# Low parts of weights made by an accumulating DMA instead of a subtraction, in a two-layer decoder trunk

## The chip, the cores and the metric

One core of a Trainium2 chip runs the kernel. The metric is the device time of one execution in microseconds (us), the lower the better. The profile names the engines PE (TensorE, matrix products; PEld is its weight load), DVE (VectorE), ACT (ScalarE), POOL (GpSimd) and SP (SyncE, which here only issues DMAs).

## The reference

A decoder trunk of two layers works on 512 tokens of 1024 features in fp32. Layer 0 mixes a gated linear recurrence with a sparse attention, layer 1 is multi-head latent attention. Both end alike:

```python
h = layer_norm(DN_ALPHA * x + m, ln1_g[i], ln1_b[i])            # m: the mixer's output
f = jnp.square(jax.nn.relu(h @ mlp_w1[i])) @ mlp_w2[i]          # 1024 -> 4096 -> 1024
e = jax.nn.sigmoid(h @ ple_w_gate[i]) * (p[i] @ ple_w_proj[i])
x = layer_norm(DN_ALPHA * h + f + e, ln2_g[i], ln2_b[i])
```

Layer 1 begins with a down-projection and makes its queries from it:

```python
down = x @ w_down                                               # 1024 -> 512 + 256 + 32
cq, ckv, kr = jnp.split(down, [MLA_Q_LORA, MLA_Q_LORA + MLA_KV_LORA], axis=-1)
q = (rms_norm(cq, q_norm) @ w_uq).reshape(bsz, s, MLA_HEADS, MLA_NOPE + MLA_ROPE)
...
q_rope = rope(q_rope, cos[:, None, :], sin[:, None, :])
```

## The kernel before, in words

Activations lie transposed, features on the 128 partitions and 512 tokens along the free dimension, eight tiles of 128 features. A product in fp32 quality is made of three products in the faster fp32r type: each operand is split into a high part `hi`, its value rounded to fp32r, and a low part `lo`, the value less `hi`. `mm3` (lines 106 to 109) adds hi x hi (line 107), hi x the activation's lo (108) and the weight's lo x hi (109) in PSUM; lines 916 to 918 and 977 to 979 do the same in the other orientation.

`wload` (lines 92 to 104) brings one weight block of 128x2048, 1 MB, from HBM into a tile `wraw` by a DMA on SP's queue, and `split` makes the parts in two pieces of 128x1024 (in four where `pieces=4`): ScalarE casts the piece into `whi` (line 89), then VectorE, or GpSimd where `sub=nc.gpsimd.tensor_sub`, subtracts `whi` from `wraw` into `wlo` (line 90). The tiles `wraw`, `whi` and `wlo` have two buffers each, shared by all weights of the kernel. A buffer of `whi` and `wlo` comes free when TensorE has done the last product with the block before the last, a buffer of `wraw` when its last split has read it, and only then can SP issue the next load into it.

The order of instructions on each engine is made when the program is built, by a list scheduler that goes by priorities and its own estimates of time; it keeps dependencies, not the order of the code. `high_priority(ahead)` puts the splits of a block that many places forward. On the chip each engine works through its own list in order.

The feed-forward (`mlp`, line 848) runs in four parts per layer. Each part makes 1024 of the 4096 hidden features in four blocks of `mlp_w1` by `seven` (lines 737 to 823; a form with seven products in place of eight, with splits of its own at lines 758 and 759 and a third pair of weight buffers), and multiplies them by four blocks of `mlp_w2` in `gemm_t` (line 895), adding into `y`. With eight parts there are 32 blocks of `mlp_w2`; a block takes 48 matmuls of 512 columns. In the fourth part the last block is computed in two halves of the tokens (`tail`), so that the second layer norm (`Norm`, lines 201 to 330) can begin on the first half. That norm sums on VectorE (lines 245 and 257), takes the sums to TensorE (274) and applies the result (318, 319, 327, 328; line 330 on GpSimd).

Layer 1's mixer begins with `group_n` (lines 905 to 920) for `w_dn0` (512 columns) and `w_dn1` (288 columns), each in two blocks of four pieces with GpSimd subtracting, and goes on with the rotary weight `w_qr` (line 971), one block of two pieces, also with GpSimd.

Of the kernel before, what the change touches and what calls it, by code (L numbers as in the profile page):

```python
# [12 lines left out]
OP = mybir.AluOpType  # L13

P = 128
S = 512
# [37 lines left out]
def hybrid_kernel(ctx: ExitStack, tc: tile.TileContext, a: dict, out: bass.AP):  # L54
    nc = tc.nc
    uid = [0]

    def nm(s):
        uid[0] += 1
        return f"{s}_{uid[0]}"  # L60

    def pool(name, bufs=2):
        return tc.tile_pool(name=name, bufs=bufs, reuse_waits="tile")
# [6 lines left out]
    def f(ap):  # L70
        return ap.bitcast(F32)
# [16 lines left out]
    def split(hi, lo, src, act=None, sub=None):  # L88
        (act or nc.scalar.copy)(hi, src)  # L89
        (sub or nc.vector.tensor_sub)(lo, src, f(hi))  # L90

    def wload(dram, idx, n=2048, pieces=2, sub=None, raw=None, ahead=30):

        hi = wp.tile([P, 2048], F32R, tag="whi", name=nm("whi"))
        lo = wp.tile([P, 2048], F32R, tag="wlo", name=nm("wlo"))
        if raw is None:
            raw = wp.tile([P, 2048], F32, tag="wraw", name=nm("wraw"))
            nc.sync.dma_start(raw[:, :n], dram[idx, :, :n])
        m = n // pieces
        with tc.high_priority(ahead):  # L100
            for i in range(pieces):
                c = slice(i * m, (i + 1) * m)
                split(hi[:, c], lo[:, c], raw[:, c], sub=sub)
        return hi, lo

    def mm3(ps, whi, wlo, xhi, xlo, start, stop):
        nc.tensor.matmul(ps, whi, xhi, start=start, stop=False)  # L107
        nc.tensor.matmul(ps, whi, xlo, start=False, stop=False)  # L108
        nc.tensor.matmul(ps, wlo, xhi, start=False, stop=stop)  # L109
# [1 line left out]
    ALL, HALVES = slice(0, S), (slice(0, H), slice(H, S))  # L111

    def gemm_t(dram, idxs, xs, evac, kk=8, nt=2, lead=0, ps=ps_tile, sub=None, loaded=None,
               halves=(), tail=0, ahead=30):

        tiles = {}  # L120

        def part(g, c, w, kn, cs=ALL):
            ktot = kk * len(idxs[g])
            for k, n in kn:
                key = g, n, cs.start
                if key not in tiles:
                    tiles[key] = ps()
                kx = c * kk + k
                hi, lo = xs[kx]
                o = slice((k * nt + n) * P, (k * nt + n + 1) * P)  # L130
                mm3(tiles[key][:, cs], w[0][:, o], w[1][:, o], hi[:, cs], lo[:, cs],
                    kx == 0, kx == ktot - 1)
                if kx == ktot - 1:
                    evac(g * nt + n, tiles[key], cs)

        first, last = 0, len(idxs) - tail
        byn = [(k, n) for n in range(nt) for k in range(kk)]
        byk = [(k, n) for k in range(kk) for n in range(nt)]
        if lead:
            w = loaded or [wload(dram, idxs[g][0], sub=sub, ahead=ahead) for g in range(2)]  # L140
            first = 2
            for cs in HALVES if "lead" in halves else (ALL,):
                for k in range(lead):
                    for g in range(2):
                        part(g, 0, w[g], [(k, n) for n in range(nt)], cs)
                for g in range(2):
                    kn = (byk, byn)[g]
                    part(g, 0, w[g], [t for t in kn if t[0] >= lead], cs)
        for g in range(first, last):
            for c, idx in enumerate(idxs[g]):  # L150
                part(g, c, wload(dram, idx, sub=sub, ahead=ahead), byn)
        if tail:
            w = {(g, c): wload(dram, idx, sub=sub, ahead=ahead) for g in range(last, len(idxs)) for c, idx in enumerate(idxs[g])}
            for cs in HALVES:
                for g in range(last, len(idxs)):
                    cn = [(c, n) for n in range(nt) for c in range(len(idxs[g]))]
                    for c, n in cn if cs.start == 0 else sorted(cn):
                        part(g, c, w[g, c], [(k, n) for k in range(kk)], cs)
# [12 lines left out]
    for k in range(KT):  # L171
        c = slice(k * 256, (k + 1) * 256)
# [283 lines left out]
    def mixer0(mixed):  # L456
        with pool("m0", 1) as m0, pool("m0s") as sc:
# [58 lines left out]

            kt = []
            gemm_t(a["w_in"], [[1], [0]], x, ev0, lead=8, loaded=w0)


# [327 lines left out]
    def mlp(layer, norm1, pp, mp):  # L848
        h, xb, pools = norm1.h, [], ExitStack()
        third = pools.enter_context(pool(f"third{layer}"))  # L850


        def evg(n, ps, cs):
            sg = mp.tile([P, S], F32, tag=f"ah{n % 2}", bufs=1, name=nm("sg"))[:, cs]
            nc.scalar.activation(sg, ps[:, cs], AF.Tanh, scale=0.5)
            nc.vector.scalar_tensor_tensor(pp[n][:, cs], sg, 1.0, pp[n][:, cs], op0=OP.add, op1=OP.mult)
            if n == 3 and cs.start:
                xb.extend(norm1.sums(mp))
            for i in range(4) if n == 3 and cs.start else (n,) if n > 3 else ():
                nc.vector.scalar_tensor_tensor(y[i], y[i], ALPHA, pp[i], op0=OP.mult, op1=OP.add)  # L860

        gemm_t(a["w_gate"], [[layer * 4 + g] for g in range(4)], h, evg, lead=8, halves=("lead",), ahead=120)
        for part in range(4):
            act = []

            def ev1(g, c11, t):
                nc.scalar.activation(t[:, :H], c11, AF.Relu)
                nc.scalar.activation(t[:, H:], t[:, H:], AF.Relu)
                nc.scalar.activation(t, t, AF.Square)
                for i in range(2):  # L870
                    n, r = 2 * g + i, t[:, i * S:(i + 1) * S]
                    hi = mp.tile([P, S], F32R, tag=f"ah{n}", bufs=1, name=nm("ah"))
                    lo = mp.tile([P, S], F32R, tag=f"al{n}", bufs=1, name=nm("al"))
                    split(hi, lo, r)
                    act.append((hi, lo))

            seven(a["mlp_w1"], [layer * 16 + part * 4 + g for g in range(4)], xb, mp, ev1, third=third)

            def ev2(n, ps, cs):
                yn = y[n][:, cs]  # L880
                if part == 0:
                    nc.vector.scalar_tensor_tensor(yn, ps[:, cs], norm1.ab[:, n:n + 1], yn, op0=OP.add, op1=OP.add)
                else:
                    nc.vector.tensor_add(yn, yn, ps[:, cs])  # L884
                if part == 3:
                    if n == 3:
                        norm.first()
                    elif n > 3:
                        norm.add(n, cs)

            if part == 3:
                pools.close()
                norm = Norm(pools.enter_context(pool(f"norm{layer}b", 1)), layer, 1, final=layer == 1)
            b = (layer * 2 + part // 2) * 8 + part % 2
            gemm_t(a["mlp_w2"], [[b + 2 * g] for g in range(4)], act, ev2, tail=part == 3)
        pools.close()
        return norm.h


    def mixer1(x1, mixed):  # L900
        with pool("m1", 1) as m1, ExitStack() as pools:
# [3 lines left out]
            def group_n(dram, ncols, xs, evac):  # L905

                ps = [ps_tile() for _ in range(NB)]
                w = [[u[:, :4 * ncols].rearrange("p (k n) -> p k n", n=ncols)
                      for u in wload(dram, ci, 4 * ncols, pieces=4, sub=nc.gpsimd.tensor_sub)] for ci in range(2)]
                for half in range(2):  # L910
                    for k in range(KT):
                        for b in (2 * half, 2 * half + 1):
                            c = slice(b * P, (b + 1) * P)
                            o = ps[b][:, :ncols]
                            (hi, lo), (whi, wlo) = xs[k], (u[:, k % 4] for u in w[k // 4])
                            nc.tensor.matmul(o, hi[:, c], whi, start=k == 0, stop=False)  # L916
                            nc.tensor.matmul(o, hi[:, c], wlo, start=False, stop=False)  # L917
                            nc.tensor.matmul(o, lo[:, c], whi, start=False, stop=k == KT - 1)  # L918
                    for b in (2 * half, 2 * half + 1):
                        evac(b, ps[b])  # L920
# [47 lines left out]


            qr = m1.tile([P, NB, MLA_H, 32], F32, tag="qr", name="qr")  # L970
            whi, wlo = (w.rearrange("p (k n) -> p k n", n=S) for w in wload(a["w_qr"], 0, sub=nc.gpsimd.tensor_sub))
            for b in range(NB):
                ps = ps_tile()
                c = slice(b * P, (b + 1) * P)
                for k in range(4):
                    hi, lo = cq[k]
# [241 lines left out]
```

## Time and profile before

| | |
|---|---|
| median of 3 runs (lowest, highest) | 1265.72 us (1263.74, 1266.52) |
| the profiled execution: its time, its span | 1267.45 us, 1265.7 us |
| busy: PE, DVE, ACT, POOL | 1225.8, 924.4, 667.1, 167.4 us |
| mean granted clock of PE | 0.990 |

The span runs from the first to the last instruction of the profiled execution. Busy time is the sum over an engine's instructions; engines work side by side, so these don't add up. The granted clock is TensorE's, as a share of 2.4 GHz; its lower level is 1.2 GHz. In a row `out<-in` are the program's names for tiles, `L90` is line 90, and in brackets stands how long the engine was idle before an instruction and what ended that.

### The profile page before, as it was taken

Reading aid. Unit: us, or ns where it says so; the run is one execution under the profiler, and the core shown is the slowest. Engines: PE = TensorE matmul, PEld = TensorE weight load, DVE = VectorE, ACT = ScalarE, POOL = GpSimd, SP = SyncE. Lnnn points to the kernel's source line nnn. Section 1 sums busy time; section 2 is a strip of 40 time slices with the busy share of each in tenths; the row PEclk is TensorE's granted clock in tenths of the full one; section 3 lists DMA queues with packets and bytes.
Section 4 is the critical chain, followed back from the end, with each engine's and each line's share of the span. In section 5 each row is a group of like instructions: output and inputs, shape, how many; then the busy total and the mean of one; then the engine's idle time right before and its main releaser. Section 6 shows DMA issues by size and latency. Waiting matters only on the chain.

```text
span 1265.7 us, 18749 instructions
## 1 busy us (share of the span) xinstructions
PE 1225.8 (97%) x7240; PEld 1063.4 (84%) x7240; DVE 924.4 (73%) x1793; ACT 667.1 (53%) x1216; POOL 167.4 (13%) x202
## 2 busy tenths in 40 slices
PE   8898899999999999999899999999999999999998
PEld 6744678989899898897797888799898998988987
DVE  5998867998566575586838788579985674855857
ACT  4594664656335254364356888446563362542633
POOL 0501660000000000000544553300000000000000
PEclk9998899999999999999999999999999999999999
DMA  6211122122323314123113111122232231231311
GB/s 217 101 33 67 67 76 75 68 101 100 126 75 134 100 67 134 67 101 133 38 68 117 51 51 51 50 85 83 100 134 97 70 133 68 100 134 67 134 34 68
DMA packets 22457, 113.07 MB, mean 89 GB/s; under 512 B 2976, under 2 KB 7072, under 8 KB 10176
## 3 DMA queue, kind: packets, MB, share of 16 engines
q1 hardware_dynamic: 22272, 111.28, 25.6%
q8 instruction: 57, 0.93, 0.3%
q0 software_dynamic: 96, 0.59, 0.2%
q14 instruction: 32, 0.26, 0.1%
HBM read 107.66 MB, written 2.10 MB: 87 GB/s over the span
## 4 chain that ended last, share of the span: by engine, by line
PE 81%; DVE 12%; ACT 3%; issue 1%; POOL 1%; DMA 1%; ACTq 0%; SPq 0%; POOLq 0%; DVEq 0%
PE ps L793 26%; PE ps L107 15%; PE ps L108 15%; PE ps L109 15%; DVE mb L551 2%; DVE m L550 2%; PE ps L397 2%; PE ps L417 1%; ACT whi L89 1%; PE ps L1095 1%; PE ps L917 1%; PE ps L918 1%; PE ps L916 1%; PE ps L1096 1%; DVE xc L611 1%
## 5 line engine op out<-in xcount | busy, mean ns | idle before, releaser
L89 ACT CAST whi<-wraw 128x1024 fp32r<-128x1024 f32 (+3 forms) x154 | 129.9, 882 | 151.2 <-PE ps L108 118.3
L107 PE MATMUL ps<-ah,whi 128*128 128x512 f32 (+1 forms) x544 | 206.4, 379 | 0.0
L108 PE MATMUL ps<-al,whi 128*128 128x512 f32 (+1 forms) x544 | 206.4, 379 | 0.0
L109 PE MATMUL ps<-ah,wlo 128*128 128x512 f32 (+1 forms) x544 | 205.3, 377 | 0.0
L107 PE MATMUL ps<-hh,whi 128*128 128x256 f32 (+1 forms) x432 | 147.1, 343 | 6.7 <-ACT hh L89 5.2
L109 PE MATMUL ps<-hh,wlo 128*128 128x256 f32 (+1 forms) x432 | 145.4, 340 | 1.4 <-DVE wlo L90 0.8
L108 PE MATMUL ps<-hl,whi 128*128 128x256 f32 (+1 forms) x432 | 146.5, 340 | 0.0
L90 POOL TENSOR_TENSOR wlo<-wraw,whi 128x512 fp32r<-128x512 f32 (+2 forms) x46 | 72.8, 1605 | 472.8 <-ACT whi L89 440.3
L90 DVE TENSOR_TENSOR wlo<-wraw,whi 128x1024 fp32r<-128x1024 f32 (+1 forms) x108 | 115.6, 1102 | 19.9 <-ACT whi L89 19.7
L793 PE MATMUL ps<-xt,whi 128*128 128x256 f32 x680 | 124.6, 284 | 0.0
L108 PEld LDWEIGHTS ps<-al,whi 128*128 128x128 f32 x544 | 102.8, 189 | 20.1 <-DVE al L90 1.2
L107 PEld LDWEIGHTS ps<-ah,whi 128*128 128x128 f32 x544 | 102.8, 189 | 19.5 <-ACT ah L89 1.1
L109 PEld LDWEIGHTS ps<-ah,wlo 128*128 128x128 f32 x544 | 102.8, 189 | 18.6 <-issue 0.5
L793 PEld LDWEIGHTS ps<-xt,whi 128*128 128x128 f32 x680 | 106.0, 192 | 0.4
L758 ACT CAST whi<-wraw 128x1024 fp32r<-128x1024 f32 (+1 forms) x43 | 36.0, 837 | 130.8 <-PE ps L108 89.6
L884 DVE TENSOR_TENSOR y<-y,ps 128x512 f32<-128x512 f32 (+1 forms) x52 | 33.3, 644 | 94.7 <-PE ps L109 94.6
L793 PE MATMUL ps<-xt,wlo 128*128 128x256 f32 x340 | 96.2, 283 | 0.0
L107 PEld LDWEIGHTS ps<-hh,whi 128*128 128x128 f32 x432 | 82.7, 192 | 16.1 <-ACT hh L89 5.2
L109 PEld LDWEIGHTS ps<-hh,wlo 128*128 128x128 f32 x432 | 82.5, 192 | 11.3 <-DVE wlo L90 2.0
L108 PEld LDWEIGHTS ps<-hl,whi 128*128 128x128 f32 x432 | 82.9, 192 | 8.7 <-DVE hl L90 0.6
L793 PE MATMUL ps<-hh,wlo 128*128 128x256 f32 x260 | 73.5, 283 | 0.0
L793 PE MATMUL ps<-hl,whi 128*128 128x256 f32 x260 | 73.5, 283 | 0.0
(335 smaller groups left out, 2951.7 us busy)
## 6 DMA issues: line engine op xcount, KB each, us to landing
wraw<-in_mlp_w SPq DMA_DIRECT2D x64, 1024.0 KB, 4.8
wraw<-in_w_out SPq DMA_DIRECT2D x8, 1024.0 KB, 5.1
wraw<-in_w_gate SPq DMA_DIRECT2D x8, 1024.0 KB, 4.7
wraw<-in_w_in SPq DMA_DIRECT2D x6, 1024.0 KB, 4.7
wraw<-in_w_ukv SPq DMA_DIRECT2D x4, 1024.0 KB, 4.7
wraw<-in_w_in SPq DMA_DIRECT2D x16, 128.0 KB, 5.0
y<-in_xT SPq DMA_DIRECT2D x8, 256.0 KB, 3.6
wraw<-in_w_proj SPq DMA_DIRECT2D x2, 1024.0 KB, 4.9
```

The lines of the kernel that those rows point to most:

```text
L89: (act or nc.scalar.copy)(hi, src)
L90: (sub or nc.vector.tensor_sub)(lo, src, f(hi))
L107: nc.tensor.matmul(ps, whi, xhi, start=start, stop=False)
L108: nc.tensor.matmul(ps, whi, xlo, start=False, stop=False)
L109: nc.tensor.matmul(ps, wlo, xhi, start=False, stop=stop)
L397: nc.tensor.transpose(ps[t][:, c:c + P], self.L[blk][:, kb * P:(kb + 1) * P], ident)
L417: nc.tensor.matmul(po[:, c], v, hi, start=kb == 0, stop=kb == NB - 1)
L550: nc.vector.max(out=m8, in_=src)
L551: nc.vector.match_replace(out=w, in_to_replace=m8, in_values=src, imm_value=LOWEST)
L758: nc.scalar.copy(hi, src)
L793: nc.tensor.matmul(o, u[:, c], v, start=start and k == n == 0, stop=k == 3 and n == 2, skip_group_check=True)
L884: nc.vector.tensor_add(yn, yn, ps[:, cs])
```

## The change: low parts as negated high parts plus an accumulating DMA

With `adds=True`, `wload` makes the low part in another way: ScalarE casts the piece into `whi` as before, ScalarE then writes `whi` times -1 into `wlo`, and a DMA issued by GpSimd adds the piece of `wraw` to `wlo` in SBUF. No subtraction on VectorE or GpSimd is left for such a block. It is used for all 32 blocks of `mlp_w2`, both blocks each of `w_dn0` and `w_dn1`, and `w_qr`; there `ahead` goes from 30 to 60, and the down-projection's blocks are cut into two pieces instead of four. All other weights stay as they are.

```diff
-    def wload(dram, idx, n=2048, pieces=2, sub=None, raw=None, ahead=30):
+    def wload(dram, idx, n=2048, pieces=2, sub=None, raw=None, ahead=30, adds=False):
...
         with tc.high_priority(ahead):
             for i in range(pieces):
                 c = slice(i * m, (i + 1) * m)
-                split(hi[:, c], lo[:, c], raw[:, c], sub=sub)
+                if adds:
+                    nc.scalar.copy(hi[:, c], raw[:, c])
+                    nc.scalar.mul(lo[:, c], f(hi[:, c]), -1.0)
+                    nc.gpsimd.dma_start(f(lo[:, c]), raw[:, c], accum_op=OP.add)
+                else:
+                    split(hi[:, c], lo[:, c], raw[:, c], sub=sub)
         return hi, lo
...
     def gemm_t(dram, idxs, xs, evac, kk=8, nt=2, lead=0, ps=ps_tile, sub=None, loaded=None,
-               halves=(), tail=0, ahead=30):
+               halves=(), tail=0, ahead=30, adds=False):
...
-                part(g, c, wload(dram, idx, sub=sub, ahead=ahead), byn)
+                part(g, c, wload(dram, idx, sub=sub, ahead=ahead, adds=adds), byn)
...
-            gemm_t(a["mlp_w2"], [[b + 2 * g] for g in range(4)], act, ev2, tail=part == 3)
+            gemm_t(a["mlp_w2"], [[b + 2 * g] for g in range(4)], act, ev2, tail=part == 3, ahead=60, adds=True)
...
-                      for u in wload(dram, ci, 4 * ncols, pieces=4, sub=nc.gpsimd.tensor_sub)] for ci in range(2)]
+                      for u in wload(dram, ci, 4 * ncols, ahead=60, adds=True)] for ci in range(2)]
...
-            whi, wlo = (w.rearrange("p (k n) -> p k n", n=S) for w in wload(a["w_qr"], 0, sub=nc.gpsimd.tensor_sub))
+            whi, wlo = (w.rearrange("p (k n) -> p k n", n=S) for w in wload(a["w_qr"], 0, ahead=60, adds=True))
```

The loads of the last blocks of a part (`tail`) pass `adds` on in the same way.

## Rows read from the trace of the kernel before

**Rows 1.** The page: busy us and share of the span by engine.

```profile
PE 1225.8 (97%) x7240; PEld 1063.4 (84%) x7240; DVE 924.4 (73%) x1793; ACT 667.1 (53%) x1216; POOL 167.4 (13%) x202
```

**Rows 2.** Stretches: length, busy us of each engine (instructions), TensorE's granted clock, DMA.

```profile
317.60:361.20 43.60, 43.60 (x194) 35.88 (x193) 23.14 (x29) 12.62 (x15) 0.00 (x0) 1.00 0.35 121
277.10:317.60 40.50, 40.50 (x337) 40.25 (x337) 36.09 (x59) 25.07 (x39) 0.00 (x0) 1.00 0.31 105
```

**Rows 3.** TensorE's waits: us in total, times, longest.

```profile
PE ps L274 <- DVE n_s L245: 5.1, 2, 3.0
...
PE ps L109 <- DVE wlo L90: 0.8, 1, 0.8
```

**Rows 4.** VectorE's timeline, second norm of layers 0 and 1: start us, us.

```profile
605.97 1.77 DVE L257 TENSOR_TENSOR n_s<-n_s,n_sq 128x512 f32<-128x512 f32 x1
...
1239.42 0.69 DVE L257 TENSOR_TENSOR n_s<-n_s,n_sq 128x512 f32<-128x512 f32 x1
```

**Rows 5.** GpSimd's timeline in the norm of layer 0.

```profile
604.20 6.39 POOL L90 TENSOR_TENSOR wlo<-wraw,whi 128x512 fp32r<-128x512 f32 x4 [414.59 <-ACT whi L89]
```

**Rows 6.** Stretches behind TensorE's two waits, columns as in rows 2.

```profile
613.38:621.46 8.08, 8.08 (x55) 8.08 (x56) 5.01 (x17) 1.52 (x4) 1.27 (x2) 0.79 0.01 5
...
631.47:645.20 13.73, 13.73 (x55) 11.78 (x56) 8.76 (x26) 4.67 (x13) 2.69 (x6) 0.75 0.01 2
```

**Rows 7.** Groups of instructions by shape: busy us, mean ns.

```profile
L90 DVE TENSOR_TENSOR wlo<-wraw,whi 128x1024 fp32r<-128x1024 f32 x92 | 109.4, 1220 | 12.4 <-ACT whi L89 12.2
...
L869 ACT ACTIVATE c<-c 128x1024 f32<-128x1024 f32 x32 | 33.8, 1058 | 0.3
```

**Rows 8.** DMA: a queue's packets, MB, share; issues, KB each, us to landing.

```profile
q1 hardware_dynamic: 22272, 111.28, 25.6%
...
wraw<-in_mlp_w SPq DMA_DIRECT2D x64, 1024.0 KB, 4.8
...
q<-hh SPq DMA_DIRECT2D x9, 64.0 KB, 2.0
...
q<-in_aug POOLq DMA_DIRECT2D x1, 512.0 KB, 5.8
gr<-in_gates SPq DMA_DIRECT2D x1, 512.0 KB, 3.4
```

**Rows 9.** ScalarE's timeline: casts of weight blocks to their high parts.

```profile
313.36 2.00 ACT L89 CAST whi<-wraw 128x1024 fp32r<-128x1024 f32 x2 [1.10 <-PE ps L793]
...
328.58 2.01 ACT L89 CAST whi<-wraw 128x1024 fp32r<-128x1024 f32 x2 [6.04 <-PE ps L108]
...
391.56 2.00 ACT L89 CAST whi<-wraw 128x1024 fp32r<-128x1024 f32 x2
...
651.07 1.42 ACT L89 CAST whi<-wraw 128x288 fp32r<-128x288 f32 x4
...
660.42 2.00 ACT L89 CAST whi<-wraw 128x1024 fp32r<-128x1024 f32 x2 [1.34 <-issue]
```

**Rows 10.** TensorE's timeline: matmuls of the weight blocks.

```profile
317.60 0.40 PE L107 MATMUL ps<-ah,whi 128*128 128x512 f32 x1
...
318.06 0.39 PE L109 MATMUL ps<-ah,wlo 128*128 128x512 f32 x1
...
322.15 0.42 PE L107 MATMUL ps<-ah,whi 128*128 128x512 f32 x1
322.41 0.39 PE L109 MATMUL ps<-ah,wlo 128*128 128x512 f32 x1
...
339.94 0.39 PE L109 MATMUL ps<-ah,wlo 128*128 128x512 f32 x1
...
401.56 0.40 PE L107 MATMUL ps<-ah,whi 128*128 128x512 f32 x1
...
653.94 0.29 PE L917 MATMUL ps<-wlo,hh 128*128 128x288 f32 x1
...
665.81 0.39 PE L978 MATMUL ps<-wlo,cq 128*128 128x512 f32 x1
```

More of the change, by code (lines that the diff above doesn't have):

```diff
@@ L150, in gemm_t @@
             for c, idx in enumerate(idxs[g]):
-                part(g, c, wload(dram, idx, sub=sub, ahead=ahead), byn)
+                part(g, c, wload(dram, idx, sub=sub, ahead=ahead, adds=adds), byn)
         if tail:
-            w = {(g, c): wload(dram, idx, sub=sub, ahead=ahead) for g in range(last, len(idxs)) for c, idx in enumerate(idxs[g])}
+            w = {(g, c): wload(dram, idx, sub=sub, ahead=ahead, adds=adds) for g in range(last, len(idxs)) for c, idx in enumerate(idxs[g])}
             for cs in HALVES:
```

## The prediction

> **What bounds the kernel now.** I read the page first: TensorE is busy for 97% of the span [rows 1]. The busy time by stretches then shows where the rest is. In the feed-forward TensorE has no gap at all: 43.60 us busy of the 43.60 of one second product, 40.50 of 40.50 in the first product before it, at clock 1.00 [rows 2]. Nothing that VectorE saves there can shorten the span; work on ScalarE, GpSimd or a DMA is free there until a low part comes late. The list of TensorE's waits gives the places where time can be won: 5.1 us in two waits of the second norm's statistics for VectorE's sums, against 0.8 us for low parts of weights [rows 3]. Both long waits lie between layer 0 and layer 1, at 610.4 and 629.4 us.
>
> Why is VectorE late there? In layer 0 three additions of 128x512 in a row take 1.77, 1.78 and 1.77 us (one is shown); the same instruction in layer 1 takes 0.69 [rows 4]. What differs is GpSimd: from 604.20 to 610.59 us it subtracts the low parts of the first down-projection block [rows 5]. In layer 1 nothing follows and GpSimd is idle. So these subtractions cost VectorE about 3 x 1.08 = 3.2 us on the path that sets the end. After each of the two waits TensorE's granted clock fell: 0.79 over 8.08 us and 0.75 over 13.73 us [rows 6], which is part of the time at 1.2 GHz instead of 2.4.
>
> **What the change removes.** 64 VectorE subtractions of 128x1024 at 1.22 us (of the group of 92 [rows 7]), 78 us, all under a TensorE without gaps: worth 0. And GpSimd's subtractions for w_dn0, w_dn1 and w_qr, of which those of w_dn0 slow VectorE on the path.
>
> Gain at the first wait: the 2.96 us of it (3.0 in [rows 3]) are less than the 3.2 us of slowing, so I take all of it, and the low clock behind it, 8.08 x (1 - 0.79) = 1.7 us: 4.7 us. At the second: 2.1 us of wait and 13.73 x 0.25 = 3.4 us of clock, 5.5 us; there GpSimd also runs other work of the norm (line 330) that stays, and the second block of w_dn0 comes later than now. I take half, 2.75, between 0 and 5.5. Together -7.4 (bounds -4.7 and -10.2).
>
> **What it adds.** On ScalarE one multiplication per piece: a 128x1024 ACTIVATE from SBUF takes 1.06 us [rows 7], 64 x 1.06 = 68 us in the feed-forward. ScalarE is busy for 12.62 us of 43.60 in a second product and 25.07 of 40.50 in a first one [rows 2]; 8.5 us per part fit. Behind the multiplications on ScalarE's queue stand the squares and casts that make the last activations of a part; TensorE has 36 matmuls of the first block (8.2 us at 43.60 / 192 = 0.227) that don't need them. Worth 0, bound about 1 us a part.
>
> On GpSimd's queue 64 + 10 DMAs. In the feed-forward GpSimd does nothing [rows 2], so a DMA that waits there for its multiplication holds up nobody.
>
> On the DMA engines 64 adds of 512 KB and 10 smaller ones. No row shows an adding DMA. Below, a 64 KB copy from SBUF to SBUF lands after 2.0 us; a 512 KB load on SP's queue takes 3.4 us, one of the same size issued by GpSimd 5.8 us [rows 8]. Above, twice the last, since source and destination are both read: 11.6 us. I take 5.8, queue and size being the same. By the Trainium skill ("DMA: Bandwidth & Descriptors", section on the anatomy of a DMA on the gpsimd path) a DMA costs some 2.0 us plus its bytes at 436 GB/s, and its "Collectives: The Full Stack" (why ReduceScatter is half of AllGather) charges an add for two source reads; estimated from both, 2.0 + 2.4 = 4.4 us, and lateness below would be 1.4 us less each time. No run shows either yet.
>
> **Is a low part ready in time?** New chain: buffer free, cast 1.0 (two in 2.00 [rows 9]), multiply 1.06, DMA 5.8: 7.9 us for the first half block.
>
> - Third and fourth blocks of a part: the buffer comes free at 328.58 [rows 9], the low part is first read at 339.94 [rows 10]: 11.4 us. Slack 3.5 us; an add may take 9.3 us.
> - The weight's own buffer is now held until the add has landed, so the load of the block after next starts later. First block cast at 313.36; its second half lands at 313.36 + 4.1 + 5.8 = 323.3, a load takes 4.8 [rows 8], so 328.1 against 328.58: just in time. In such a part the add may take 7.8 us before the third block's low part is late (two adds follow each other in that chain).
> - First block of a part: in five of the eight parts its buffer comes free 10 us ahead (391.56 against 401.56), enough. In three (313.36, and the same distance at 565.27 and 1114.97 us) only 4.2 us ahead: cast at 313.36, first product at 317.60, first low part read at 318.06 [rows 9, 10]. The new chain ends at 321.3, 3.2 us late. The cover is the order of the matmuls: it is not tied to the order of the code (at 322.15 a hi product stands ahead of an outstanding low one [rows 10]), and hi products of the first six k for two outputs are 24 x 0.227 = 5.4 us. Between 0 and 3.2 us each I take 0.7, near the cover: 3 x 0.7 = 2.1.
> - Second block of w_dn1: cast at 651.07, first read 653.94 [rows 9, 10]. Its pieces are 576 wide, twice the 288 of that row: 0.7 + 0.7 and, between 3.4 and 5.8, some 4 us: 656.5, 2.5 late. Cover: 24 products of the first block, 3.1 us at 288/512 of 0.227. I take 1.0.
> - w_qr: cast at 660.42, read at 665.81 [rows 9, 10]; new 660.42 + 7.9 = 668.3, 2.5 late, with 32 products without low parts behind it. ScalarE is busy there with the norm of q, so I take the middle, 1.3.
>
> Sum: -7.4 + 2.1 + 1.0 + 1.3 = -3.0 against the profiled execution's 1267.45 us: 1264.4. That execution lies 1.7 us above the median of the runs shown, 1265.72; moved to the median, 1262.7 us.
>
> **Rivals.** A measurement of this kernel can tell about 0.2%, 2.5 us, from no change.
>
> *Even.* The second wait stays, because it hangs on GpSimd's remaining work and on the later low part of w_dn0's second block: -4.7 + 4.4 = -0.3, 1265.4 us. For it: line 330 runs on GpSimd in that stretch too. Against: the subtractions of the first block slow VectorE's additions to more than twice their time [rows 4].
>
> *Slower: the first blocks stall.* In the three short parts the hi products are not put ahead, TensorE waits 3.2 us each time and loses clock as after its present wait of 2.96 us (1.7 each): 1262.7 - 2.1 + 9.6 + 5.1 = 1275.3 us. It decides at an add of 2.6 us without reordering, at 8.0 us with it. For it: an order fixed when the program is built helps only as far as the lateness was foreseen. Against: the order at 322 us.
>
> *Slower: the adds are slow.* From 9.3 us an add makes the third and fourth blocks late, 16 blocks. At the upper bound of 11.6 that is 16 x 2.3 = 37 us and 11 us in the first blocks, near 1310 us; at 10 us about 1280. The DMA engines as such are far from full: loads of 111.28 MB take 25.6% of the span [rows 8], 2.9 us per MB; a block's load and its add, read twice, make 8.7 us of the 10.9 us that TensorE spends on it. An add that costs them four times a load would make it 14.5 us, and then they are the bound. By the Trainium skill ("DMA: Bandwidth & Descriptors", issuing engines are not separate DMA queues) loads and adds share the same 16 engines, whichever engine issues them.
>
> *It doesn't do what it says*: the low parts cost VectorE nothing, yet its slow additions stay slow, GpSimd not being their cause. Then only the costs are left, 1265.72 + 4.4 = 1270 us; the comparison of the two layers speaks against it.
>
> **How the numbers follow.** Forecast 0.43 (its own range 1257.6, all of the gain at only 2.1 of cost, to 1263.2), even 0.24, first blocks 0.18, slow adds 0.11, no relief 0.04. Faster 0.43, same 0.24, slower 0.33. For 8 in 10 the range runs from 1256 to 1278, over the stalling first blocks, and leaves out the slow adds and the edges.
>
> **What would show it.** Right: the three additions at the norm of layer 0 at 0.69 us, TensorE's wait for the sums under 0.5 us, clock near 1.00 behind it, no wait of the matmuls of line 109 for a low part, 5 to 6 us from an add's issue to its landing. Wrong: new waits of line 109 for the DMA at 318, 570 and 1119 us or at the third blocks, a clock under 1.00 in the feed-forward, or ScalarE's table load and column means (lines 199 and 236) pushed back by multiplications at 592 and 1226 us, which would delay the norm by up to 2 us.

## The result and the profile after

The changed kernel is slower: a median of 1282.01 us (1277.42 to 1283.46, 4 runs) against 1266.12 us (1263.74 to 1269.54, 4 runs) of the kernel before on the same chip. The ratio is 1.0111, 95% interval 1.0087 to 1.0134, so +14 us (11 to 17). The two medians by themselves lie 15.9 us apart; differences in us are taken from the ratios here, so they are good to 2 or 3 us and no better. The forecast was 1262.7 us in a range of 1256 to 1278. The profiled execution took 1277.42 us, span 1275.6; it is the quickest of the four and shows 9.9 us of the rise.

Line numbers of the changed kernel are higher by 6 from the new lines on: 274 is now 280, 109 is 115, 917 is 923. Its cast, multiplication and adding DMA are lines 105, 106 and 107. First the page: busy time by engine, the DMA queues (packets, MB, share of 16 engines), and DMA issues (KB each, median us to landing); beside [rows 1, 8].

```profile
PE 1228.9 (96%) x7240; PEld 1061.0 (83%) x7240; DVE 844.0 (66%) x1729; ACT 732.8 (57%) x1282; POOL 208.2 (16%) x258
...
q1 hardware_dynamic: 22272, 111.28, 26.0%
q0 software_dynamic: 10752, 38.47, 15.5%
...
wraw<-in_mlp_w SPq DMA_DIRECT2D x64, 1024.0 KB, 4.9
wlo<-wraw POOLq DMA_DIRECT2D x70, 512.0 KB, 6.3
```

VectorE has 80 us less to do, ScalarE 66 more. The adds are the queue q0, all but 0.6 MB of it; their median of 6.3 us is near the 5.8 that was taken. On the average nothing looks wrong. The waits of TensorE (us in total, times, longest) tell it:

```profile
PE ps L923 <- DMA wlo<-wraw: 5.9, 4, 3.2
PE ps L115 <- DMA wlo<-wraw: 5.3, 6, 1.5
...
PE ps L983 <- ACT kr L963: 1.2, 1, 1.2
PE ps L984 <- DMA wlo<-wraw: 0.8, 1, 0.8
```

The 5.1 us for the norm's sums [rows 3] are gone, and these four lines make 13.2 us of waits, of which the kernel before had 0.2 (for `kr`). Their places: lines 115 at 320 and 323 us (first part), 574 (fourth), 1129, 1142 and 1151 us (seventh); line 923 at 628 (second block of `w_dn0`) and at 647 to 657 us (`w_dn1`); lines 983 and 984 at `w_qr`.

The relief at the norm is as forecast. VectorE's timeline has the addition of [rows 4] at 0.69 us in layer 0 too:

```profile
608.90 0.69 DVE L263 TENSOR_TENSOR n_s<-n_s,n_sq 128x512 f32<-128x512 f32 x1
```

Stretches of the profiled execution (length, busy us of PE, PEld, DVE, ACT, POOL, granted clock, DMA share, GB/s): the second product of the first part, the ten microseconds with the norm's additions, the stretch behind the norm's first half, the one behind the wait at 657 us, and the one behind the waits at `w_qr`.

```profile
315.91:362.08 46.17, 44.45 (x195) 35.81 (x193) 15.86 (x23) 18.19 (x21) 6.29 (x8) 1.00 0.79 205
...
603.40:613.40 10.00, 10.00 (x72) 9.31 (x70) 9.42 (x18) 6.31 (x10) 1.72 (x2) 1.00 0.78 197
...
613.40:620.18 6.78, 6.78 (x55) 6.58 (x56) 4.96 (x17) 1.51 (x4) 1.27 (x2) 1.00 0.73 151
...
657.39:663.00 5.61, 5.61 (x32) 5.61 (x33) 0.33 (x2) 2.99 (x11) 0.00 (x0) 0.73 0.57 188
...
668.28:675.00 6.72, 5.89 (x17) 4.01 (x17) 4.04 (x9) 5.79 (x11) 3.98 (x4) 0.75 0.68 130
```

Behind the norm's first half the clock is 1.00 where it was 0.79 [rows 6]; but it is now 0.73 and 0.75 in two stretches of the down-projection and of `w_qr`, and the feed-forward, once without a gap [rows 2], has 1.72 us idle in its first second product, at clock 1.00. Measured from the first matmul of a stage to that of the next, the fourth part's second product with the norm gained 2.4 us, and the rest lost: the first part 2.5, the seventh 3.7, the down-projection 4.1, the stage from `w_qr` to the next feed-forward 2.8, the other five parts 0.1 to 0.2 each. The beginning, where nothing was changed, was 1.7 us shorter. A stage's time in a single execution can't be read finer than that: in two runs below that leave the down-projection as it was before (`w2_only`, `short_first`) it is 1.6 and 3.0 us shorter than in the kernel before, by the clock (last section).

**Why the first block of a short part is late.** ScalarE's, GpSimd's and TensorE's timelines at the first part, where [rows 9, 10] show the kernel before:

```profile
311.67 2.00 ACT L105 CAST whi<-wraw 128x1024 fp32r<-128x1024 f32 x2 [1.10 <-PE ps L799]
313.57 2.00 ACT L106 ACTIVATE wlo<-whi 128x1024 fp32r<-128x1024 f32 x2
...
331.73 2.00 ACT L105 CAST whi<-wraw 128x1024 fp32r<-128x1024 f32 x2 [9.13 <-DMA wraw<-in_mlp_w]
```

```profile
315.22 1.85 POOL L107 DMA_DIRECT2D wlo<-wraw  x2 [127.25 <-DVE c L826]
```

```profile
317.91 0.40 PE L114 MATMUL ps<-al,whi 128*128 128x512 f32 x1
319.77 0.50 PE L115 MATMUL ps<-ah,wlo 128*128 128x512 f32 x1 [1.47 <-DMA wlo<-wraw]
```

The chain from cast to low part takes 319.77 - 311.67 = 8.1 us; 7.9 were worked out. That they agree is luck, since the pieces don't: ScalarE does both casts before the first multiplication (1.90 us where 1.0 was taken), from the multiplication's start to the add's issue pass 1.65 us instead of 1.06, and the add itself takes 4.55 instead of 5.8. TensorE begins the block at 315.91 us, the same 4.24 us behind the cast as before, but puts only eight matmuls (four k, lines 113 and 114) ahead of the first low product, 1.9 us, where 24 were counted on.

**Why later blocks are late.** The third row of ScalarE above says the next thing: the third block's cast waits for its load. It starts 15.8 us into the product, against 11.0 before (328.58 - 317.60). The same happens in the seventh part. SP's issue of the third block's load, in the kernel before and in the changed one (second products from 1119.21 and from 1125.21 us):

```profile
1118.44 0.33 SPq L98 DMA_DIRECT2D wraw<-in_mlp_w  x1
```

```profile
1131.45 0.33 SPq L99 DMA_DIRECT2D wraw<-in_mlp_w  x1
```

The DMA issues of two short stretches, 1130 to 1132 us and 1142 to 1146 us, show what it then meets:

```profile
wraw<-in_mlp_w SPq DMA_DIRECT2D x1, 1024.0 KB, 8.5
wlo<-wraw POOLq DMA_DIRECT2D x1, 512.0 KB, 11.3
...
wraw<-in_mlp_w SPq DMA_DIRECT2D x1, 1024.0 KB, 6.1
wlo<-wraw POOLq DMA_DIRECT2D x2, 512.0 KB, 8.6
```

The load of the third block could be issued only when the first block's adds had landed, at 1131.45 us, 6.2 into the product; before, the same load went out 0.8 us ahead of it. So it meets the second block's last add: the load takes 8.5 us and the add 11.3, issued at 1131.17 and awaited by TensorE until 1142.47. That is the second block's second half; the third block's first low part, cast behind the late load, is awaited until 1151.17. The 6.3 us of the page are a median over quiet and crowded places.

### The profile page after: what moved, and what is told of

The parts are those of the page before. It is cut to its first block, busy times and chain, and to the rows that moved or that the text cites. A ratio compares the mean times of both kernels' runs of the same rounds, so it can differ in the third digit from the quotient of the medians.

```text
span 1275.6 us, 18984 instructions
## 1 busy us (share of the span) xinstructions
PE 1228.9 (96%) x7240; PEld 1061.0 (83%) x7240; DVE 844.0 (66%) x1729; ACT 732.8 (57%) x1282; POOL 208.2 (16%) x258
## 3 DMA queue, kind: packets, MB, share of 16 engines
q0 software_dynamic: 10752, 38.47, 15.5%
## 4 chain that ended last, share of the span: by engine, by line
PE 80%; DVE 10%; DMA 4%; ACT 3%; issue 1%; POOL 1%; ACTq 0%; SPq 0%; POOLq 0%; DVEq 0%
PE ps L799 25%; PE ps L115 14%; PE ps L113 14%; PE ps L114 14%; DMA wlo<-wraw 3%; DVE mb L557 2%; PE ps L403 2%; DVE m L556 2%; PE ps L423 1%; PE ps L1101 1%; PE ps L1102 1%; PE ps L1103 1%; PE ps L923 1%; DMA wraw<-in_mlp_w 1%; PE ps L924 1%
## 5 line engine op out<-in xcount | busy, mean ns | idle before, releaser
L107 POOL DMA_DIRECT2D wlo<-wraw x74 | 63.8, 870 | 807.4 <-ACT wlo L106 658.5
L105 ACT CAST whi<-wraw 128x1024 fp32r<-128x1024 f32 (+1 forms) x74 | 73.2, 1025 | 118.7 <-PE ps L114 82.1
L113 PEld LDWEIGHTS ps<-hh,whi 128*128 128x128 f32 x432 | 82.5, 192 | 15.9 <-ACT hh L89 5.2
L764 ACT CAST whi<-wraw 128x1024 fp32r<-128x1024 f32 (+1 forms) x43 | 35.9, 836 | 100.6 <-PE ps L114 68.1
L115 PEld LDWEIGHTS ps<-hh,wlo 128*128 128x128 f32 x432 | 82.1, 191 | 11.2 <-DVE wlo L90 2.0
L89 ACT CAST whi<-wraw 128x1024 fp32r<-128x1024 f32 (+2 forms) x72 | 55.8, 812 | 38.8 <-PE ps L114 25.4
L106 ACT ACTIVATE wlo<-whi 128x1024 fp32r<-128x1024 f32 (+1 forms) x74 | 74.0, 1029 | 0.1
```

The source lines that it names most:

```text
L105: nc.scalar.copy(hi[:, c], raw[:, c])
L106: nc.scalar.mul(lo[:, c], f(hi[:, c]), -1.0)
L107: nc.gpsimd.dma_start(f(lo[:, c]), raw[:, c], accum_op=OP.add)
L764: nc.scalar.copy(hi, src)
```

## The experiments

Diffs are against the changed kernel, "as before" means the form of the kernel before. Every ratio is to the kernel before. All kernels compute the whole reference.

**The adds of `mlp_w2` alone** (`w_dn0`, `w_dn1` and `w_qr` as before).

```diff
-                      for u in wload(dram, ci, 4 * ncols, ahead=60, adds=True)] for ci in range(2)]
+                      for u in wload(dram, ci, 4 * ncols, pieces=4, sub=nc.gpsimd.tensor_sub)] for ci in range(2)]
...
-... wload(a["w_qr"], 0, ahead=60, adds=True))
+... wload(a["w_qr"], 0, sub=nc.gpsimd.tensor_sub))
```

> Adds for the 32 blocks of mlp_w2 alone; the down-projection and rotary weights are as before the change. Theory (a low part is late where its buffer comes free shortly before its use): the feed-forward's share of the loss is the three short parts, in the changed kernel's profile about 2.5 + 1.1 + 3.7 us; here 6 to 9 us slower than before, TensorE's waits for the norm's sums (3.0 and 2.1 us) are back, and all waits for an adding DMA lie at the first three blocks of those three parts. Rival (adds crowd the loads off the DMA engines): over 10 us, with waits in all eight parts.

Measured: 1277.31 us, ratio 1.0093 (1.0068 to 1.0118), +11.8 us. TensorE's waits:

```profile
PE ps L115 <- DMA wlo<-wraw: 6.2, 8, 1.5
...
PE ps L280 <- DVE n_s L251: 5.0, 2, 2.9
```

The feed-forward, where nothing could be won, costs most of the rise. All eight waits lie in first to third blocks of the three short parts; the five long parts have none and are 0.1 to 0.2 us longer. So the places are the theory's, but the loss is above its 6 to 9 us, in the range of the rival, whose waits in all eight parts did not come. The two waits of the norm are back, as they should be.

**Everything but `mlp_w2`.**

```diff
-            gemm_t(a["mlp_w2"], [[b + 2 * g] for g in range(4)], act, ev2, tail=part == 3, ahead=60, adds=True)
+            gemm_t(a["mlp_w2"], [[b + 2 * g] for g in range(4)], act, ev2, tail=part == 3)
```

> Adds for the down-projection and rotary weights alone; mlp_w2 is as before the change. Theory: the two waits for the norm's sums go (about 5 us gained with the clock behind them), the second block of each down-projection weight and w_qr come late (about 8 us lost): 2 to 5 us slower than before. Rival (adds crowd the loads): nothing else loads much here, so at most 1 us from before, or a gain.

Measured: 1268.77 us, 1.0020 (1.0007 to 1.0034), +2.5 us. The norm's waits are gone, but what came at the down-projection and at `w_qr` costs more than that: waits of 1.61, 0.78 and 3.13 us for `w_dn0` and `w_dn1`, of 1.22 and 0.82 us at `w_qr`.

**The first block of `w_dn0` alone** (`mlp_w2` and `w_qr` as before, too).

```diff
+                      for u in (wload(dram, ci, 4 * ncols, ahead=60, adds=True) if ncols == 512 and ci == 0 else
+                                wload(dram, ci, 4 * ncols, pieces=4, sub=nc.gpsimd.tensor_sub))] for ci in range(2)]
```

> Adds for the first block of w_dn0 alone, whose buffer comes free some 15 us before its use. Theory: the first wait for the norm's sums goes (3.0 us, and the low clock behind it), nothing comes late: 3 to 6 us faster than before. Rival (GpSimd's subtractions don't cause VectorE's slow additions, or any gain is given back further on): within 1 us of before.

Measured: 1262.62 us, 0.9966 (0.9956 to 0.9976), -4.3 us. The first of the norm's waits is gone, VectorE's additions take 0.68 to 0.69 us, and the second wait stays at 2.11 us:

```profile
608.08 0.69 DVE L263 TENSOR_TENSOR n_s<-n_s,n_sq 128x512 f32<-128x512 f32 x1
```

```profile
PE ps L280 <- DVE n_s L251: 2.1, 1, 2.1
```

GpSimd's subtractions of this one block were the cause of the first.

**Both blocks of `w_dn0` alone** (the condition is `ncols == 512`).

> Adds for both blocks of w_dn0 and for nothing else. It prices the second block, whose buffer comes free when TensorE begins on the first. Theory (late where the buffer comes free shortly before use): TensorE waits some 1.6 us for that block's low part, as in the run with all three weights, but the second wait for the norm's sums (2.1 us) goes: 1 to 5 us faster than before, 0 to 4 us slower than with the first block alone. Rival (the second block's add costs nothing, all of the loss there is w_dn1's and w_qr's): as fast as with the first block alone or faster, no wait for a DMA in the down-projection.

Measured: 1260.00 us, 0.9942 (0.9922 to 0.9961), -7.4 us. Both waits of the norm are gone and one of 1.61 us for the second block's add has come. It was expected to be up to 4 us slower than the first block alone and is 3 us faster:

```profile
PE ps L924 <- DMA wlo<-wraw: 1.6, 1, 1.6
```

**Both blocks of `w_dn0` and of `w_dn1`** (`mlp_w2` and `w_qr` as before).

> Adds for w_dn0 and w_dn1, none for w_qr and mlp_w2. It parts the loss behind w_dn0: with w_dn0 alone the kernel was 7.5 us faster than before, with all three 2.5 us slower. Theory (w_dn1's second block, read 3 us after its buffer comes free, is the worst placed): of these 10 us some 6 are w_dn1's, so 0 to 3 us faster than before, a wait of about 3 us at the second block of w_dn1. Rival (w_qr's multiplications on ScalarE and its late low part): 5 us or more faster than before.

Measured: 1265.34 us, 0.9977 (0.9967 to 0.9986). Against the run with `w_dn0` alone, `w_dn1` costs 0.9977 - 0.9942 = 0.35%, 4.4 us; against the run with `w_qr`, `w_qr` costs 1.0020 - 0.9977 = 0.43%, 5.5 us; by the intervals either is uncertain by 2 to 3 us. Waits of 0.77 and 2.41 us at `w_dn1` stay. By the medians `w_dn1` costs 4.4 us as well, and `w_qr` 4.5.

**The changed kernel without the three short first blocks** (their low parts by VectorE).

```diff
-                part(g, c, wload(dram, idx, sub=sub, ahead=ahead, adds=adds), byn)
+                part(g, c, wload(dram, idx, sub=sub, ahead=ahead, adds=adds and not (skip and g == 0)), byn)
...
+                   skip=(layer, part) in ((0, 0), (0, 3), (1, 2)))
```

> The changed kernel, but the first block of mlp_w2 in the three short parts is split by VectorE again; 29 blocks of mlp_w2 still use the adds. Theory: the waits for an adding DMA in the feed-forward go, and with them 5 to 8 us of the loss; what stays is the down-projection's, so 2 to 6 us slower than before. Rival (adds crowd the loads): with 29 of 32 adds left, at least 9 us slower than before.

Measured: 1273.98 us, 1.0059 (1.0037 to 1.0080), +7.5 us, between what the theory and the rival expected. With the adds of 29 of the 32 blocks left, one wait of 0.46 us is all that TensorE has for them, at the fourth block of a part that is not short:

```profile
PE ps L115 <- DMA wlo<-wraw: 0.5, 1, 0.5
```

So the waits at the second and third blocks of the short parts, too, came from the adds of the short first blocks: in the seventh part the third block's load goes out at 1125.28 us, once more 0.8 us ahead of the product, and an add takes 4.4 us and a load 4.8 (medians of 1115 to 1160 us). The time is 0.39%, 5 us, above the run without any add of `mlp_w2`, though; between their profiled executions the stages show 1.3 us at that one wait, 1.7 at the down-projection (its longest wait is 3.99 us instead of 3.13) and 0.1 to 0.2 in the other parts. Why the adds of `mlp_w2` make a wait at the down-projection longer stays open.

**The three short first blocks alone** (`adds=adds and skip and g == 0`; all else as before).

> Adds for the first block of mlp_w2 in the three short parts alone, every other weight as before the change. Theory (this block's own low part is late): waits for the adding DMA of 1 to 1.5 us in each of the three parts and nowhere else, 3 to 6 us slower than before. Rival (it takes the adds of the blocks behind it as well: the weight's buffers held by one add after another, and two adds and a load at once on the DMA engines): at most 2 us slower, the 10 us of the run with all 32 blocks come only when they stand together.

Measured: 1273.65 us, 1.0036 (1.0026 to 1.0046), +4.6 us. Waits of 1.47, 1.15 and 1.16 us at these blocks, nowhere else:

```profile
PE ps L115 <- DMA wlo<-wraw: 3.8, 3, 1.5
```

In the seventh part an add takes 5.4 us here and a load 5.2 (medians of 1115 to 1155 us), against 7.9 and 7.8 with all of `mlp_w2`: the crowding needs the adds of the first block and of those behind it together. The blocks' own lateness is 4.6 of the 11.8 us.

**VectorE instead of the DMA** (`mlp_w2`: ScalarE multiplies, VectorE adds; all else as before).

```diff
-                    nc.gpsimd.dma_start(f(lo[:, c]), raw[:, c], accum_op=OP.add)
+                    nc.vector.tensor_add(lo[:, c], raw[:, c], f(lo[:, c]))
```

> Adds for mlp_w2 alone as in the run before, but VectorE adds wraw to the negated high part in place of the DMA. ScalarE's load is the same, no DMA is added and the buffer of wraw comes free as early as before. Theory: the loss was the adds' landing, so at most 2 us slower than before. Rival (ScalarE's 64 multiplications hold up the last activations of a part): 6 us or more slower, with TensorE waiting for ah at the start of the second products.

Measured: 1266.32 us, 0.9997 (0.9981 to 1.0013). ScalarE's 64 multiplications cost nothing that this run can tell (by the interval -2.4 to +1.6 us); what `mlp_w2` costs comes from the DMA, by its time or by the source that it holds.

**Multiplication before the second cast** (the changed kernel; the order on ScalarE is forced).

```diff
-                    nc.scalar.copy(hi[:, c], raw[:, c])
-                    nc.scalar.mul(lo[:, c], f(hi[:, c]), -1.0)
+                    with tc.issue_after(neg.ins) if i else ExitStack():
+                        nc.scalar.copy(hi[:, c], raw[:, c])
+                    neg = nc.scalar.mul(lo[:, c], f(hi[:, c]), -1.0)
```

> The changed kernel with one order tied down: ScalarE multiplies a piece right behind its cast instead of after both casts, so the first add of a block starts 1.0 us earlier and the second as before. Theory of lateness: each stall that waits for the first half of a block shrinks by up to 1 us; some six places, so 2 to 6 us faster than the changed kernel, that is 8 to 14 us slower than before. Rival (what limits is the rate of the DMA engines, both halves share it and the second half still lands when it did): within 1.5 us of the changed kernel.

Measured: 1291.74 us, 1.0188 (1.0170 to 1.0207), +23.8 us where 8 to 14 were expected. The first wait fell only from 1.47 to 1.13 us, and new ones of 4.21 and 3.49 us came at the ends of the first and the seventh part. ScalarE's and TensorE's timelines at the first of these:

```profile
352.26 0.62 ACT L765 CAST wh<-wraw 128x512 fp32r<-128x512 f32 x1 [7.01 <-DMA wraw<-in_mlp_w]
353.59 1.57 ACT L765 CAST wh<-ws 128x1024 fp32r<-128x1024 f32 x2 [0.71 <-DVE ws L782]
355.07 1.06 ACT L107 ACTIVATE wlo<-whi 128x1024 fp32r<-128x1024 f32 x1
```

```profile
360.84 0.79 PE L116 MATMUL ps<-ah,wlo 128*128 128x512 f32 x1 [4.21 <-DMA wlo<-wraw]
```

The fourth block's last multiplication now stands on ScalarE's list behind a cast of the next part's weight, which waits 7 us for its load. The run changed more of the order than was meant, so what the order cast, cast, multiply costs by itself stays open.

**The first block of `w_dn0` and two early blocks of `w_out0`**, another place where GpSimd subtracts beside VectorE, ahead of the first feed-forward.

```diff
-                        wo.append(wload(a["w_out0"], len(wo), sub=nc.gpsimd.tensor_sub, ahead=0))
+                        wo.append(wload(a["w_out0"], len(wo), ahead=0, adds=True))
```

> Adds for the first block of w_dn0 and for the two blocks of w_out0 that are loaded during the sparse attention of layer 0, long before their use, and whose subtractions GpSimd makes today ahead of its own scaling of the attention rows (a wait of 1.8 us of TensorE). Theory: an add pays where the block has time and GpSimd's subtraction stands in the way: 1 to 3 us faster than with the first block of w_dn0 alone, so 6 to 8 us faster than before. Rival (only the norm's place matters): as fast as the first block of w_dn0 alone, 5 us faster than before, the wait of 1.8 us still there.

Measured: 1256.72 us, 0.9920 (0.9903 to 0.9938), -10.1 us, more than the 6 to 8 expected. The gain is not where the expectation looked for it: the wait of 1.8 us for GpSimd's scaling is still there, as the rival had it, but TensorE's wait for VectorE falls from 6.0 to 2.5 us (a new one of 0.9 us for an add comes). In the run with the first block of `w_dn0` alone, GpSimd's subtraction for `w_out0` takes 5.12 us from 132.59 us on, and three instructions of VectorE that run beside it take 2.30, 2.83 and 1.64 us; here the subtraction is gone and they take 0.69, 0.68 and 0.69. One of them, there and here:

```profile
135.43 2.83 DVE L657 SCALAR_TENSOR_TENSOR rc<-s,rc 128x512 f32<-128x512 f32 x1
```

```profile
133.37 0.68 DVE L657 SCALAR_TENSOR_TENSOR rc<-s,rc 128x512 f32<-128x512 f32 x1
```

**Both blocks of `w_dn0` and the two of `w_out0`.**

> The two edits that paid, together: adds for both blocks of w_dn0 and for the two early blocks of w_out0, nothing else. If their gains lie at different places and add up (7.5 us and, beyond the first block of w_dn0, 5.9 us): 12 to 15 us faster than before, 1253 to 1256 us. Rival (the gains are one and the same, or one gives back what the other wins): 8 to 11 us faster, as the better of them alone.

Measured: 1257.11 us, 0.9902 (0.9885 to 0.9918), -12.4 us: with the run above, from which the intervals don't part it, the quickest here and ahead of both kernels. Its waits:

```profile
PE ps L403 <- DVE mn L386: 2.4, 1, 2.4
...
PE ps L924 <- DMA wlo<-wraw: 1.6, 1, 1.6
PE ps L115 <- DMA wlo<-wraw: 1.0, 1, 1.0
```

**The same with the later blocks of `w_ukv`.**

```diff
-                w = wload(a["w_ukv"], g, pieces=4, sub=nc.gpsimd.tensor_sub)
+                w = (wload(a["w_ukv"], g, ahead=60, adds=True) if g else
+                     wload(a["w_ukv"], g, pieces=4, sub=nc.gpsimd.tensor_sub))
```

> As the run with both blocks of w_dn0 and w_out0, and adds also for the blocks of w_ukv loaded during the latent attention, which GpSimd and VectorE split today. Theory (only a wait of TensorE can be won): TensorE has hardly a gap there, so within 2 us of that run. Rival (every subtraction taken from GpSimd frees VectorE and pays): 3 us or more faster than that run.

Measured: 1259.03 us, 0.9919 (0.9905 to 0.9934). No gain over the run above, as expected: TensorE did not wait for these low parts before, so there was nothing to win, and the stage is 2.2 us longer in the profile, with new waits of 1.48 and 1.29 us for ScalarE's casts.

## Why the prediction was wrong

The gain was right in place and mechanism, and in size with some luck. The costs were summed at 4.4 us and measured about 21.7. The pieces, -7.4 (`w_dn0`), +4.4 (`w_dn1`), +5.5 (`w_qr`) and +11.8 us (`mlp_w2`), add up to +14.3; the changed kernel measured +14. The two in the middle are differences of runs, so this is in effect the sum of two runs, +2.5 and +11.8; by the medians the same two give 11.2 of 15.9 us, and the run without the short first blocks lies 5 us above the one without any add of `mlp_w2`, with hardly a wait in the feed-forward to show for it. The order of the costs is shown, a microsecond of any one is not.

**The norm's two waits: right.** Summed at -4.7 and -2.75; measured -4.3 with the first block and -7.4 with both. That the half taken for the second wait fits the 3.1 us measured is luck: the wait did not stay by half, it vanished, and the add of `w_dn0`'s second block, which the sum named and did not price, took 1.61 us back. The 3.4 us of clock counted in for it are those of one execution, too (last section). GpSimd's subtraction beside VectorE's additions is shown as the cause, since taking one block of it away switched the additions from 1.77 to 0.69 us, and the same switch at `w_out0` did the like to three other instructions. The Trainium skill ("SBUF — State Buffer", section on who interferes with whom) says that a VectorE instruction with two SBUF inputs contends with a GpSimd instruction that reads SBUF, while a DMA never contends with a compute engine; the additions at 0.69 us in a stretch where adds and loads kept the DMA engines 78% busy (603.40 to 613.40 us) agree with both.

**VectorE's relief and ScalarE's load worth 0 in the feed-forward: right.** The run with VectorE adding, which has ScalarE's load alone, gave 0.9997; the five long parts, where VectorE is relieved and no low part is late, are no shorter than before.

**The first blocks of the three short parts: the step that failed.** "Between 0 and 3.2 us each I take 0.7, near the cover." The chain came out right to 0.2 us, though not in its pieces; the cover was not. Twenty-four hi products were counted as free to go ahead of the first low one, from a single place at 322 us where one did; the order that was built puts eight ahead. That is the rival of the stalling first blocks, and its lateness of 3.2 us less 1.9 of cover gives the waits of 1.1 to 1.5 us that came. The term was 2.1 us and measured 4.6. The clock stayed at 1.00 in the feed-forward's stretches that were read, against that rival's 1.7 us each. Why the scheduler put no more ahead was not tried.

**An add as a fixed 5.8 us: the second failure, and the larger one.** The chain for the third block was drawn up ("a load takes 4.8 [rows 8], so 328.1 against 328.58: just in time") with the add and the load each at its time alone. That the held buffer puts the load off was foreseen (issued at 323.3, 5.7 us into the product; 6.2 came); that both then take longer because they meet was not: 8.5 us for the load, 11.3 for the add. Without adds in the short first blocks the load goes out ahead and the waits are gone. For this the sum had nothing; by the ratios it is some 7 of the 11.8 us that `mlp_w2` costs. The profiled executions show less of it: against the run with the short first blocks alone, the three short parts are 3.7 us longer, of which 2.4 are waits, and the five others 0.7 together, without a wait; where the rest is stays open. Whether a third buffer of `wraw`, which would take the hold away and leave the sharing, mends it was not tried.

**`w_dn1`: 1.0 us taken, 4.4 measured.** The same fault. Adds of 288 KB were put at some 4 us; the first block's two, alone on the engines, took 3.6. The second block's are issued beside the load of `w_qr`, as the DMA issues between 648 and 650.5 us show (the two adds took 4.0 and 8.3 us, and TensorE's wait ended with the slower):

```profile
wraw<-in_w_qr SPq DMA_DIRECT2D x1, 1024.0 KB, 6.5
wlo<-wraw POOLq DMA_DIRECT2D x2, 288.0 KB, 6.2
```

The cast came earlier than forecast, 7.9 us ahead of the moment at which TensorE ran out of other work (646.34 against 654.21; 2.9 us were worked out), and the low part was late all the same: from cast to first use the chain took 657.39 - 646.34 = 11.0 us where 5.4 were worked out. TensorE waited 3.18 us, and then ran at 0.73 for 5.61 us, 1.5 us more. (Of the ten adds outside the feed-forward only these four are smaller than 512 KB, not all ten as the prediction says; no term hung on it.)

**`w_qr`: 1.3 us taken, 5.5 measured.** Here ScalarE's queue, which "is busy there with the norm of q", was named and had no price of its own; the middle between none and all of the lateness was taken:

```profile
662.21 2.01 ACT L105 CAST whi<-wraw 128x1024 fp32r<-128x1024 f32 x2
664.11 2.01 ACT L106 ACTIVATE wlo<-whi 128x1024 fp32r<-128x1024 f32 x2
666.02 0.38 ACT L932 ACTIVATE junk<-ps 128x256 f32<-128x256 f32 x1
```

```profile
668.28 0.84 PE L983 MATMUL ps<-whi,cq 128*128 128x512 f32 x2 [1.18 <-ACT kr L963]
669.95 0.50 PE L984 MATMUL ps<-wlo,cq 128*128 128x512 f32 x1 [0.83 <-DMA wlo<-wraw]
```

The chain took 669.95 - 662.21 = 7.7 us, near the 7.9 worked out, but the multiplications push the norm of q behind them, so that even the hi products wait (1.18 us, before 0.20), then the low part is late (0.83), and the clock behind is 0.75 over 6.72 us (1.7): 3.7 us of the 5.5 can be read off.

**The rivals.** "Even" and "no relief" fell with the run on `w_dn0`. "First blocks stall" was right about the place. "The adds are slow" was right that slow adds make later blocks late, but in the three short parts alone: there one of 11.3 us made the second block late, and the third was late behind its load with one of 7.8. In the five long parts the adds stay hidden, but for the one wait of 0.46 us above.

## What to carry to other kernels

A step moved to a DMA should be priced with the loads that run beside it, and with the load that its held source buffer pushes back; its time alone is the lower bound. Put such a step where the buffer comes free long before its use (in the feed-forward 10 us were enough and 4.2 were not; at `w_dn1`, beside a load, 7.9 were not), and where it ends a wait: two blocks of `w_dn0` gave all of the gain, and the other 35, taken in groups, nothing or a loss. Cover by independent matmuls counts only as far as the built order shows it at that place.

## What the runs showed of the hardware

An add inside SBUF moves half the bytes per second of a load. The DMA view of the first part, 305 to 330 us in 40 slices (busy tenths, GB/s), and the time of the low parts' DMAs there:

```profile
DMA  9499900000100000005999999999999969999998
GB/s 210 184 419 459 393 13 0 0 0 0 26 0 0 0 0 0 0 0 98 210 216 210 197 210 216 210 177 210 216 210 190 210 138 282 315 282 315 301 315 288
```

```profile
DMA to landing us min/median/max: 4.5/6.7/9.6
```

Loads reach 393 to 459 GB/s at the start; from the 20th slice on the adds alone fill the engines at 210, and with a load among them it is about 300. Over the span the adds cost 15.5% of 1275.6 us for 38.47 MB, 5.1 us per MB; the loads cost 3.0. By the Trainium skill ("Collectives: The Full Stack", why ReduceScatter is half of AllGather) an add needs two source reads and so half the rate, which the 210 against some 420 GB/s bears out. The estimate of 4.4 us from it and from "DMA: Bandwidth & Descriptors" holds for an add with little beside it (4.5 us, the lowest here), not for one beside a load.

What a wait costs in clock is not one price. Behind the wait of 2.1 us for the sums of the norm's second half the kernel before had 0.75 over 13.73 us [rows 6]; in the run with the first block of `w_dn0` alone and in the one with the three short first blocks, where this wait is the same (2.11 and 2.12 us), a stretch of that length behind it reads:

```profile
628.11:641.84 13.73, 13.73 (x62) 11.78 (x63) 9.76 (x30) 6.03 (x17) 4.04 (x8) 0.88 0.01 3
```

```profile
635.68:649.41 13.73, 13.73 (x68) 11.51 (x69) 10.75 (x31) 7.43 (x20) 5.45 (x9) 1.00 0.02 6
```

TensorE gets through 55, 62 and 68 matmuls in it. So the same wait was followed by a loss of 3.4, 1.6 or 0 us, and a clock price read in one execution is good for that execution.
